# Fourth gated block multiplied ahead of the convolution's sums, and the mean's two products one group sooner

## The chip, the cores and the metric

The kernel runs on one core of a Trainium2 chip. A core has TensorE (matrix products, PE in the profile; its weight loads are listed apart as PEld), VectorE (DVE), ScalarE (ACT), GpSimd (POOL) and SyncE (SP, which issues transfers). The metric is the device time of one execution in microseconds; of several executions the median is given.

## The reference

One block of a streaming encoder, on 512 frames of width 1024: a SwiGLU half step, a mixing layer, another SwiGLU half step, an input gate and a final norm. The change lies in the mixing layer, where two branches are computed from one projection and meet in one output projection:

```python
z = _rmsnorm(h, mix_norm[i]) @ w_in[i]
conv_a, conv_gt, q, k, v, r, g_lr = jnp.split(z, SPLIT_POINTS, axis=-1)
y_conv = _conv_module(conv_a, conv_gt, conv_w[i], conv_b[i], conv_ln_g[i], conv_ln_b[i])
y_gla = _gla(q, k, v, r, g_lr, gate_w_up[i], gate_b[i], gla_norm[i])
h = h + jnp.concatenate([y_conv, y_gla], axis=-1) @ w_out[i]
...
def _conv_module(a, b, w_dw, b_dw, ln_g, ln_b):
    glu = a * jax.nn.sigmoid(b)
    y = lax.conv_general_dilated(glu, w_dw[:, None, :], ...) + b_dw      # causal, depthwise, 31 taps
    return jax.nn.silu(_layernorm(y, ln_g, ln_b))
...
# end of _gla
o = o * lax.rsqrt(jnp.mean(o * o, axis=-1, keepdims=True) + EPS)
o = o * o_norm.astype(f32).reshape(N_HEADS_GLA, HEAD_V)
return (o.reshape(bsz, seq, D_GLA_V) * jax.nn.silu(r.astype(f32))).astype(q.dtype)
```

## The kernel before

Everything is held with channels on the 128 partitions and the 512 frames along the free axis, except where frames stand on the partitions: the values `v`, the gate `r` and the attention's outputs are made in four blocks of 128 frames (`t` = 0 to 3). A product of float32 matrices is done as three products of parts: each operand is split into a high part (a rounded copy, made by ScalarE) and a low part (the rest, made by VectorE), and high x high, low x high and high x low are added up in PSUM.

Within the mixing layer the instructions of each engine run in the order in which they are written (`in_order(True)`): each engine has one queue, and an instruction that waits holds up all behind it. So the order of the lines is the order on the engines.

The lines that matter stand at the end of the mixing layer.

- The loop over `t` from line 1418 makes the gate: `tokblock(wr, t)` projects block `t` on TensorE (24 matmuls of 512 columns), and line 1438 takes its SiLU on ScalarE into `rt[t]`. After `t` = 1 ScalarE also scales the four blocks of the attention's output into `ytok` (line 1449).
- Line 1457 multiplies `ytok[i]` by `rt[i]` on VectorE: block 0 in the turn of `t` = 1, blocks 1 and 2 in that of `t` = 2, block 3 in that of `t` = 3. Between them `taps(n)` (line 1455) puts `n` turns of the convolution on VectorE.
- `taps` (line 1040) takes its turns from one or two generators, `conv_steps` (line 1027), one for each 128 channels of the convolution. A turn is one `scalar_tensor_tensor` over nearly 512 frames, `acc = glu shifted * tap + acc`; a turn that finds a generator at its end issues nothing and drops it. What is left of the taps is issued at line 1485.
- The convolution's four accumulators `acc[0..3]` are added into `acc012` (lines 1453, 1468 and 1489), since the mean over channels needs only their sum.
- Lines 1460 to 1467 transpose the four gated blocks on TensorE into `yps[0..3]`, with six products of another layer (into `pq`) among and behind them. Lines 1470 and 1471 scale and split the transposed blocks (`gsplit`: high part on ScalarE, low part on VectorE) into `mix[4..7]`.
- From there TensorE runs the output projection's half for the attention: `first_part(n, wo[n])` issues 12 matmuls, four groups `k` = 4 to 7 of three. Into `first_part(5, ...)` two products with the constant matrix `mean` are laid, one for the high part `acch` and one for the low part `accl` of `acc012` (line 1490 splits it); they leave the mean over channels, on all partitions, in the bank `mub`.
- Line 1504 subtracts it from the accumulators on VectorE, ScalarE squares them, VectorE adds the squares, and `ln_sums` (called in `first_part(3, ...)` ahead of group 6) sums them over the partitions on TensorE. `ln_out` (called in `first_part(6, ...)` ahead of group 5) spreads the root over the partitions, and the LayerNorm's output goes into `mix[0..3]`, for the other half of the output projection.

Of the kernel before, what the change touches and what calls it, by code (L numbers as in the profile page):

```python
# [12 lines left out]
ALU = mybir.AluOpType  # L13
# [49 lines left out]
def block_kernel(ctx: ExitStack, tc: tile.TileContext, a: dict, out: bass.AP):  # L63
    nc = tc.nc
    pe, dve, act, pool = (Ordered(tc, e) for e in (nc.tensor, nc.vector, nc.scalar, nc.gpsimd))
# [24 lines left out]
    def bt2(dt=F32R, s="a"):  # L90
        t = big.tile([P, 2, SEQ], dt, tag="A", bufs=NA, name=nm(s))
        hi, lo = t[:, 0], t[:, 1]
        whole_of[id(hi)] = hi, t
        return hi, lo

    def bt(dt=F32, s="a"):
        if dt not in other:
            t, other[dt] = bt2(dt, s)
            return t
        return other.pop(dt)  # L100

    def cvt(dt=F32, s="cv"):
        return big.tile([P, SEQ], dt, tag="CV", bufs=NCV, name=nm(s))
# [17 lines left out]
    def psum(pool_, n, shape, tag="mm"):  # L121
        return pool_.tile(shape, F32, tag=tag, bufs=n, name=nm("pd" if len(shape) == 3 else "ps"))

    def singles():
        return region("fixed", "spare" if mode[0] == 0 else stack[1][0] if len(stack) > 1 else "double", "singles")

    def bank():
        if mode[0] == 0:
            turn_no[0] += 1
            at = turn_no[0] % 7  # L130
            if at in (3, 4):
                return fixed()
            if at in (5, 6):
                return spare()
        return psum(singles(), 3, [P, SEQ])

    def fixed():
        return psum(region("fixed"), 2, [P, SEQ])

    def spare():  # L140
        return psum(region("fixed", "spare"), 2, [P, SEQ])
# [10 lines left out]
    def aux():  # L152
        if mode[0] == 2:
            return fixed()
        return psum(singles(), 1, [P, SEQ], "aux")
# [82 lines left out]
    def added(w):  # L238

        h3, l3, r3 = w  # L240
        act.mul(l3, r3, -1.0)
        pool.dma_start(out=l3.bitcast(F32), in_=r3, accum_op=ALU.add)
        return w
# [39 lines left out]
    def rsqrt_mean(ss, n, w, bufs=3, between=None):  # L283

        ms = tmp("ms", 16)[:, :w]
        dve.tensor_scalar(ms, ss, 1.0 / n, EPS, ALU.mult, ALU.add)
        r = tmp("rs0", 16)[:, :w]
        pool.tensor_tensor(out=r, in0=ms, in1=negh[:, :w], op=ALU.pow)
        if between is not None:
            between()  # L290
        nh = tmp("rsh", 16)[:, :w]
        dve.tensor_scalar(nh, ms, -0.5, None, ALU.mult)
        t = tmp("rs1", 16)[:, :w]
        dve.tensor_tensor(out=t, in0=r, in1=r, op=ALU.mult)
        dve.tensor_tensor(out=t, in0=t, in1=nh, op=ALU.mult)
        rs = tmp(f"rs{bufs}", 16, bufs=bufs)[:, :w]
        dve.scalar_tensor_tensor(out=rs, in0=t, scalar=1.5, in1=r, op0=ALU.add, op1=ALU.mult)
        return rs
# [152 lines left out]
    class Left:  # L451
# [17 lines left out]
        def part(self, name, engine=None):  # L469

            if name not in self.done:
                self.done[name] = low(self.cut.pop(name, None) or high(getattr(self, name)), engine or dve)
            return self.done[name]
# [518 lines left out]
    mean, mask, nbias = made  # L992
# [18 lines left out]
    glu, acc, conv = [], [cvt() for _ in range(4)], []  # L1011
# [28 lines left out]
    def taps(n):  # L1040

        for _ in range(n):
            if not conv:
                return
            i = turn[0] % min(2, len(conv))
            turn[0] += 1
            try:
                next(conv[i])
            except StopIteration:
                conv.pop(i)  # L1050
# [187 lines left out]
    def tokblock(w, t, mid={}):  # L1238

        ps = bank()  # L1240
        ts = slice(t * P, (t + 1) * P)
        i = 0
        for k in range(DC):
            wh, wl = w[k // 2][:2]
            xh, xl = hg[k]
            for x, y in ((xh, wh), (xl, wh), (xh, wl)):
                if i in mid:
                    mid[i]()
                pe.matmul(ps, x[:, ts], y[:, k % 2, :], start=(i == 0), stop=(i == 3 * DC - 1))
                i += 1  # L1250
        return ps
# [31 lines left out]
    def chunk_sums(cs):  # L1283
        for j in range(2):
            if len(kvs) == j:
                kvs.append([bank(), bank()])
            for c in cs:
                s0 = (c % 2) * CH
                for i in range(2):
                    h = 2 * j + i  # L1290
                    pe.matmul(kvs[j][c % 2][i * HK:(i + 1) * HK, (c // 2) * HV:(c // 2 + 1) * HV],
                              kdt[j][s0:s0 + CH, (c // 2) * P + i * HK:(c // 2) * P + (i + 1) * HK],
                              vt[c // 2][s0:s0 + CH, h * HV:(h + 1) * HV], start=True, stop=True)
# [18 lines left out]
    def out_of(t, h):  # L1312
        c = 2 * (t % 2) + h // 2
        return ops[2 * (t // 2) + h % 2][:, c * HV:(c + 1) * HV]
# [21 lines left out]
    def chain(cs):  # L1336
        for c in cs:
            for j in range(2):
                state(j, c)
# [39 lines left out]
    def early_parts():  # L1379
        hi, lo = (kept_p[:, i * 2 * P:(i + 1) * 2 * P].rearrange("p (k c) -> p k c", k=2) for i in range(2))  # L1380
        act.copy(hi, early_p)
        added((hi, lo, early_p))
        early_x[:] = [(hi[:, k], lo[:, k]) for k in range(2)]
        wh, wl = (wp.tile([P, 1024], F32R, tag="sm", bufs=2, name=nm("sm")).rearrange("p (k c) -> p k c", k=2)
                  for _ in range(2))
        act.copy(wh, early_w)
        early_wh[:] = added((wh, wl, early_w))[:2]
# [3 lines left out]
    def oload(n):  # L1391
        for i in range(n, n + 2):
            raw_o[i] = load(a["w_out"], 0, DC, i * P, P)

    def ohigh(n):
        return (high4 if n in (4, 5) else high)(raw_o[n])
# [14 lines left out]
    def first_part(n, w, mid={}):  # L1411
        ps = bank()
        part(ps, w, range(4, 8), True, False, mid)
        half[n] = (w, ps)

    oload(0)
    wo, rt = {n: added(ohigh(n)) for n in (0, 1)}, []
    for t in range(TB):
        if t == 0:
            ps = tokblock(wr, t, {5: lambda: chunk_sums(range(7))})  # L1420
            chain(range(7))
            taps(3)
            oload(4)
        elif t == 1:
            ps = tokblock(wr, t, {2: outputs})
            early_parts()
            taps(13)
            by_t = "p (t h) -> p t h"
            so3 = so.rearrange(by_t, h=4)
            dve.tensor_tensor(out=so3, in0=so3, in1=rs2.unsqueeze(2).to_broadcast([P, TB, 4]), op=ALU.mult)  # L1430
            rso = rsqrt_mean(so, HV * HK, 16, between=lambda: taps(5))
            rso3 = rso.rearrange(by_t, h=4)
            dve.scalar_tensor_tensor(out=rso3, in0=rso3, scalar=HK ** -0.5,
                                     in1=rs.unsqueeze(2).to_broadcast([P, TB, 4]), op0=ALU.mult, op1=ALU.mult)
        else:
            ps = tokblock(wr, t)
        r = bt(s="r")
        act.activation(r, ps, AF.Silu, scale=rs[:, t:t + 1])
        rt.append(r)
        if t == 1:  # L1440
            oload(2)
            for n in (4, 5):
                wo[n] = [added(w) for w in ohigh(n)]
            ytok = []
            for i in range(TB):
                y = bt(s="y")
                for h in range(4):
                    vs = slice(h * HV, (h + 1) * HV)
                    act.activation(y[:, vs], out_of(i, h), AF.Copy, scale=rso[:, 4 * i + h:4 * i + h + 1])
                ytok.append(y)  # L1450
        if t == 3:
            acc012 = bt(s="acc012")
            dve.tensor_tensor(out=acc012, in0=acc[0], in1=acc[1], op=ALU.add)
        if t > 0:
            taps((0, 2, 5, 1)[t])
            for i in {1: (0,), 2: (1, 2), 3: (3,)}[t]:
                dve.tensor_tensor(out=ytok[i], in0=ytok[i], in1=rt[i], op=ALU.mult)
    yps = [bank() for _ in range(4)]
    pq = bank()
    for t in range(TB):  # L1460
# [5 lines left out]
    pe.matmul(pq, early_x[0][0], early_wh[1][:, 0, :], start=False, stop=False)  # L1466
    projected(pq, 0, early_wh, early_x, (1,))
    dve.tensor_tensor(out=acc012, in0=acc012, in1=acc[2], op=ALU.add)
    taps(1)
    for h in range(4):  # L1470
        mix[4 + h] = gsplit(yps[h], vec("gla_norm", h), "yg")
    act.copy(kept_pq, pq)
# [12 lines left out]
    for steps in list(conv):  # L1485
        for _ in steps:
# [3 lines left out]
    acch, accl = split(acc012, "sum")  # L1490
# [5 lines left out]
    w1.fetch("a11", "a12")  # L1496
    first_part(4, wo[4])
    mub = aux()
    first_part(5, wo[5], {6: lambda: pe.matmul(mub, mean, acch, start=True, stop=False),
                          7: lambda: pe.matmul(mub, mean, accl, start=False, stop=True)})  # L1500
    first_part(2, wo[2])
    sqs, lln, yc = [], [], []
    for c in range(4):
# [524 lines left out]
```

## Time and profile before

| | us |
|---|---|
| median of 3 runs (921.46 to 922.23) | 922.09 |
| the profiled execution, its own time | 921.7 |
| its span | 920.0 |
| TensorE busy in 450 to 500 us, where the change lies | 49.03 of 50.00 |
| VectorE busy there | 42.34 |
| ScalarE busy there | 32.91 |
| TensorE busy in 500 to 700 us, behind it | 200.00 of 200.00 |

The span runs from the first to the last instruction of the profiled execution; the rest of its time lies around it. A row of the timeline gives start, duration, engine, line, operation, the tile written and the tiles read, and how many instructions are merged into it; in brackets stands how long the engine was idle ahead of it and which engine's instruction ended that. Nearly all instructions go through one helper, so all show its line 46, and tiles are what tells them apart. Tiles are named by the memory that they lie in: two tiles of 512 columns share one name, so that block 0 of `ytok` appears as `r`, blocks 1 to 3 as `y`, the accumulators as `cv`, and `acc012` as `r`.

### The profile page before, as it was taken

The numbers are of one execution on the slowest core, as the hardware profiler recorded it, in microseconds if no ns is written. First come the engines' busy times: TensorE is split into PE (matmuls) and PEld (weight loads), VectorE is DVE, ScalarE is ACT, GpSimd is POOL, SyncE is SP. The second block draws the span as 40 slices with busy tenths as digits, with TensorE's granted clock in tenths as the row PEclk, the third lists the DMA queues.
The fourth block names the chain that finished last, engine by engine and source line by source line (L and its number), as shares of the span: only waits on it lengthen the run. The fifth ranks groups of instructions, "written<-read, shape, count | busy, mean of one in ns | idle before, by whom it ended". The sixth has DMA issues, their size and how long they took to land.

```text
span 920.0 us, 12856 instructions
## 1 busy us (share of the span) xinstructions
PE 910.3 (99%) x4950; PEld 780.1 (85%) x4950; DVE 814.8 (89%) x1087; ACT 517.2 (56%) x755; POOL 63.7 (7%) x80
## 2 busy tenths in 40 slices
PE   9999999999999999999999999999999999999996
PEld 7899888888888887888877889888888888888885
DVE  6699989999989767999996779899999999997896
ACT  7755355445454574484675875455445444556884
POOL 0120000000000111011130020000000000000121
PEclk9999999999999999999999999999999999999998
DMA  9534334224334692267572563334224322358454
GB/s 350 185 96 140 112 112 127 89 74 137 115 91 116 154 273 76 69 122 198 138 166 93 138 160 93 115 116 128 80 90 131 121 92 84 117 155 239 93 98 132
DMA packets 37725, 119.88 MB, mean 130 GB/s; under 512 B 4256, under 2 KB 5536, under 8 KB 37664
## 3 DMA queue, kind: packets, MB, share of 16 engines
q1 hardware_dynamic: 30320, 97.48, 32.3%
q0 software_dynamic: 7200, 21.57, 12.9%
q8 instruction: 39, 0.64, 0.3%
q14 instruction: 22, 0.18, 0.1%
q10 hardware_dynamic: 144, 0.00, 0.0%
HBM read 96.43 MB, written 2.10 MB: 107 GB/s over the span
## 4 chain that ended last, share of the span: by engine, by line
PE 96%; ACT 2%; DVE 1%; DMA 0%; issue 0%; SPq 0%; POOLq 0%
PE ps L46 56%; PE pd L46 40%; DVE cv L46 1%; DMA h<-in_xT 0%; ACT wa L46 0%; ACT sq L46 0%; DVE y L46 0%; ACT r L46 0%; DVE r L46 0%; ACT sm L46 0%; ACT wh L46 0%; DVE hg L46 0%; ACT hg L46 0%; DVE lnsq L46 0%; ACT lnsq L46 0%
## 5 line engine op out<-in xcount | busy, mean ns | idle before, releaser
L46 DVE TENSOR_TENSOR wl<-wr,wh 128x1024 fp32r<-128x1024 f32 (+2 forms) x159 | 186.0, 1180 | 16.8 <-ACT wh L46 16.5
L46 ACT CAST wh<-wr 128x1024 fp32r<-128x1024 f32 (+2 forms) x177 | 175.4, 1023 | 13.3 <-PE ps L46 5.5
L46 PE MATMUL pd<-hg,wh 128*128 128x512 f32 x576 | 150.1, 392 | 0.0
L46 PE MATMUL ps<-act,wh 128*128 128x512 f32 x448 | 138.0, 390 | 0.0
L46 PEld LDWEIGHTS pd<-hg,wh 128*128 128x128 f32 x576 | 106.0, 188 | 21.0 <-DVE u L46 0.4
L46 PE MATMUL ps<-hg,wh 128*128 128x512 f32 (+1 forms) x448 | 116.8, 345 | 0.3
L46 PEld LDWEIGHTS ps<-act,wh 128*128 128x128 f32 x448 | 84.1, 188 | 17.4
L46 PE MATMUL pd<-t,wh 128*128 128x512 f32 x392 | 95.3, 392 | 0.0
L46 ACT ACTIVATE s<-g 128x512 f32<-128x512 f32 x48 | 30.4, 633 | 114.9 <-DVE g L46 114.9
L46 ACT COPY sq<-pd 128x1024 f32<-128x1024 f32 x45 | 45.8, 1017 | 86.7 <-PE pd L46 52.4
L46 PEld LDWEIGHTS ps<-hg,wh 128*128 128x128 f32 x448 | 78.1, 190 | 10.9 <-issue 0.5
L46 PE MATMUL ps<-act,wl 128*128 128x512 f32 x224 | 87.2, 390 | 0.0
L46 PEld LDWEIGHTS pd<-t,wh 128*128 128x128 f32 x392 | 71.5, 189 | 13.4
L46 PE MATMUL pd<-hg,wl 128*128 128x256 f32 (+1 forms) x544 | 81.6, 289 | 0.0
L46 PEld LDWEIGHTS pd<-hg,wl 128*128 128x128 f32 x544 | 73.9, 191 | 5.0
L46 PE MATMUL ps<-hg,wl 128*128 128x512 f32 (+1 forms) x224 | 77.1, 344 | 0.0
L46 ACT CAST wh<-sm 128x1024 fp32r<-128x1024 f32 x42 | 44.0, 1051 | 55.4 <-DVE sm L46 50.1
L46 DVE TENSOR_TENSOR wl<-sm,wh 128x1024 fp32r<-128x1024 f32 x42 | 51.1, 1220 | 5.1 <-ACT wh L46 5.1
L46 DVE TENSOR_TENSOR sq<-pd,sq 128x1024 f32<-128x1024 f32 x45 | 54.8, 1218 | 0.4 <-PE pd L46 0.4
L46 PE MATMUL ps<-wh,hg 128*128 128x512 f32 x176 | 54.5, 391 | 0.0
L46 PE MATMUL pd<-t,wl 128*128 128x256 f32 x392 | 52.5, 283 | 0.0
L46 PEld LDWEIGHTS pd<-t,wl 128*128 128x128 f32 x392 | 50.6, 192 | 1.5
(314 smaller groups left out, 1632.6 us busy)
## 6 DMA issues: line engine op xcount, KB each, us to landing
wr<-in_ffn_w_in SPq DMA_DIRECT2D x84, 512.0 KB, 3.6
wr<-in_ffn_w_out SPq DMA_DIRECT2D x32, 512.0 KB, 3.6
wl<-wr POOLq DMA_DIRECT2D x20, 512.0 KB, 5.7
wr<-in_ffn_w_out SPq DMA_DIRECT2D x16, 384.0 KB, 3.4
wr<-in_w_blocks SPq DMA_DIRECT2D x12, 512.0 KB, 5.4
wr<-in_w_rows SPq DMA_DIRECT2D x8, 512.0 KB, 4.8
wr<-in_w_out SPq DMA_DIRECT2D x8, 512.0 KB, 5.3
wq<-in_ple_w_gate SPq DMA_DIRECT2D x8, 512.0 KB, 4.2
```

The costliest lines, as they stand in the source:

```text
L46: inst = call(*args, **kwargs)
```

## The change

Three edits. Block 3 of the gate's product goes ahead of the first sum over accumulators and of the tap that stood before it; the two first sums then stand one behind the other. One tap is taken from the turn of `t` = 3 to that of `t` = 1, and the tap between the second sum and `gsplit` goes to those that are issued at line 1485. The mean's two products are laid ahead of the groups 5 and 6 of `first_part(5, ...)` instead of 6 and 7. What is computed stays the same, and so does the number of instructions on each engine.

```diff
-        if t == 3:
-            acc012 = bt(s="acc012")
-            dve.tensor_tensor(out=acc012, in0=acc[0], in1=acc[1], op=ALU.add)
         if t > 0:
-            taps((0, 2, 5, 1)[t])
+            taps((0, 3, 5, 0)[t])
             for i in {1: (0,), 2: (1, 2), 3: (3,)}[t]:
                 dve.tensor_tensor(out=ytok[i], in0=ytok[i], in1=rt[i], op=ALU.mult)
+    acc012 = bt(s="acc012")
+    dve.tensor_tensor(out=acc012, in0=acc[0], in1=acc[1], op=ALU.add)
     yps = [bank() for _ in range(4)]
...
     dve.tensor_tensor(out=acc012, in0=acc012, in1=acc[2], op=ALU.add)
-    taps(1)
     for h in range(4):
         mix[4 + h] = gsplit(yps[h], vec("gla_norm", h), "yg")
...
-    first_part(5, wo[5], {6: lambda: pe.matmul(mub, mean, acch, start=True, stop=False),
-                          7: lambda: pe.matmul(mub, mean, accl, start=False, stop=True)})
+    first_part(5, wo[5], {5: lambda: pe.matmul(mub, mean, acch, start=True, stop=False),
+                          6: lambda: pe.matmul(mub, mean, accl, start=False, stop=True)})
```

On VectorE, in the turns of `t` = 1 to 3, this stood before. `cv_3193` to `cv_3196` are the accumulators, a row with `col` is a tap; `r_4291<-r_4291,st_4145` is the product of block 0, `y_4317<-y_4317,r_4291` and `y_4317<-y_4317,y_4326` are those of blocks 1 and 2, `y_4326<-y_4326,r_4391` is that of block 3, and `r_4391<-...cv` are the sums over accumulators:

```order
L46 SCALAR_TENSOR_TENSOR cv_3195<-glu_3522,col,cv_3195 128x511
L46 TENSOR_TENSOR r_4291<-r_4291,st_4145 128x512
L46 SCALAR_TENSOR_TENSOR cv_3196<-en_3578,col,cv_3196 128x501
L46 SCALAR_TENSOR_TENSOR cv_3196<-en_3578,col,cv_3196 128x502
L46 SCALAR_TENSOR_TENSOR cv_3196<-en_3578,col,cv_3196 128x503
L46 SCALAR_TENSOR_TENSOR cv_3196<-en_3578,col,cv_3196 128x504
L46 TENSOR_TENSOR y_4317<-y_4317,r_4291 128x512
L46 TENSOR_TENSOR y_4317<-y_4317,y_4326 128x512
L46 TENSOR_TENSOR r_4391<-cv_3193,cv_3194 128x512
L46 SCALAR_TENSOR_TENSOR cv_3196<-en_3578,col,cv_3196 128x505
L46 TENSOR_TENSOR y_4326<-y_4326,r_4391 128x512
L46 TENSOR_TENSOR r_4391<-r_4391,cv_3195 128x512
```

On VectorE, at the same place, now (block 3's tiles are `y_4326` and `r_4392`):

```order
L46 SCALAR_TENSOR_TENSOR cv_3195<-glu_3522,col,cv_3195 128x511
L46 SCALAR_TENSOR_TENSOR cv_3196<-en_3578,col,cv_3196 128x501
L46 TENSOR_TENSOR r_4291<-r_4291,st_4145 128x512
L46 SCALAR_TENSOR_TENSOR cv_3196<-en_3578,col,cv_3196 128x502
L46 SCALAR_TENSOR_TENSOR cv_3196<-en_3578,col,cv_3196 128x503
L46 SCALAR_TENSOR_TENSOR cv_3196<-en_3578,col,cv_3196 128x504
L46 SCALAR_TENSOR_TENSOR cv_3196<-en_3578,col,cv_3196 128x505
L46 TENSOR_TENSOR y_4317<-y_4317,r_4291 128x512
L46 TENSOR_TENSOR y_4317<-y_4317,y_4326 128x512
L46 TENSOR_TENSOR y_4326<-y_4326,r_4392 128x512
L46 TENSOR_TENSOR r_4392<-cv_3193,cv_3194 128x512
L46 TENSOR_TENSOR r_4392<-r_4392,cv_3195 128x512
```

The tap 501 has moved ahead of block 0's product, and block 3's product stands right behind block 2's, with the first sum and the tap 505 no longer between them.

On VectorE a little later, from the last tap ahead of the four low parts `yg` to the first part of `acc012`, before:

```order
L46 SCALAR_TENSOR_TENSOR cv_3196<-en_3578,col,cv_3196 128x506
L46 SCALAR_TENSOR_TENSOR yg_4425<-ps_4396,col,yg_4425 128x512
L46 SCALAR_TENSOR_TENSOR yg_4428<-ps_4397,col,yg_4428 128x512
L46 SCALAR_TENSOR_TENSOR yg_4431<-ps_4398,col,yg_4431 128x512
L46 SCALAR_TENSOR_TENSOR yg_4434<-ps_4399,col,yg_4434 128x512
L46 SCALAR_TENSOR_TENSOR cv_3196<-en_3578,col,cv_3196 128x507
```

On VectorE, the same place, now:

```order
L46 SCALAR_TENSOR_TENSOR yg_4424<-ps_4396,col,yg_4424 128x512
L46 SCALAR_TENSOR_TENSOR yg_4427<-ps_4397,col,yg_4427 128x512
L46 SCALAR_TENSOR_TENSOR yg_4430<-ps_4398,col,yg_4430 128x512
L46 SCALAR_TENSOR_TENSOR yg_4433<-ps_4399,col,yg_4433 128x512
L46 SCALAR_TENSOR_TENSOR cv_3196<-en_3578,col,cv_3196 128x506
L46 SCALAR_TENSOR_TENSOR cv_3196<-en_3578,col,cv_3196 128x507
```

The tap 506 has moved behind the low parts; five taps stood there (507 to 511), now six, and behind them the last sum.

On TensorE, around the mean's two products (`ps_4511<-sum_4482,mean`; `ps_4512` is the bank of `first_part(5, ...)`, three matmuls a group), before:

```order
L46 MATMUL ps_4512<-yg_4425,wa_4307 128x512 x3
L46 MATMUL ps_4512<-yg_4428,wa_4307 128x512 x3
L46 MATMUL ps_4511<-sum_4482,mean 128x512
L46 MATMUL ps_4512<-yg_4431,wa_4307 128x512 x3
L46 MATMUL ps_4511<-sum_4482,mean 128x512
L46 MATMUL ps_4512<-yg_4434,wa_4307 128x512 x3
```

On TensorE, the same place, now:

```order
L46 MATMUL ps_4512<-yg_4424,wa_4307 128x512 x3
L46 MATMUL ps_4511<-sum_4482,mean 128x512
L46 MATMUL ps_4512<-yg_4427,wa_4307 128x512 x3
L46 MATMUL ps_4511<-sum_4482,mean 128x512
L46 MATMUL ps_4512<-yg_4430,wa_4307 128x512 x3
L46 MATMUL ps_4512<-yg_4433,wa_4307 128x512 x3
```

Each of the two products has moved ahead of one group of three matmuls.

## The prediction

> **What bounds the kernel now.** I read the page's busy shares and its chain of work first, then TensorE's own waits over the whole span, then the timelines of TensorE, VectorE and ScalarE around the two waits that this leaves.
>
> ```profile
> span 920.0 us, 12856 instructions
> PE 910.3 (99%) x4950; PEld 780.1 (85%) x4950; DVE 814.8 (89%) x1087; ACT 517.2 (56%) x755; POOL 63.7 (7%) x80
> PE 96%; ACT 2%; DVE 1%; DMA 0%; issue 0%; SPq 0%; POOLq 0%
> PE ps L46 <- PEq L2018: 0.8, 1, 0.8
> PE ps L46 <- DVE y L46: 0.6, 1, 0.6
> PE ps L46 <- DVE lnsq L46: 0.4, 1, 0.4
> ```
>
> TensorE is busy for 99% of the span and carries 96% of the chain that ended last. Its list of waits (total, times, longest) has three rows: the start of the program, one wait for a `y` of VectorE, one for `lnsq`. So the time falls only where TensorE stands still or does less, and the change takes no matmul away. What can be won is these last two waits.
>
> The first stands at the transposes of the gated blocks, the second at the sums of squares of the LayerNorm.
>
> ```profile
> 469.91 0.39 PE L46 MATMUL ps<-wl,hg 128*128 128x512 f32 x1
> 471.37 0.71 PE L46 MATMUL ps<-sm,up 128*128 128x512 f32 x2
> 472.69 0.66 PE L46 MATMUL ps<-ident,y 128*128 128x128 f32 x4 [0.61 <-DVE y L46]
> 474.12 0.39 PE L46 MATMUL ps<-yg,wh 128*128 128x512 f32 x1
> 474.34 0.40 PE L46 MATMUL ps<-yg,wl 128*128 128x512 f32 x1
> ...
> 489.43 0.39 PE L46 MATMUL ps<-yg,wh 128*128 128x512 f32 x1
> 490.18 1.05 PE L46 MATMUL ps<-ones,lnsq 128*128 128x1 f32 x8 [0.36 <-DVE lnsq L46]
> 491.10 0.49 PE L46 MATMUL ps<-yg,wh 128*128 128x512 f32 x1
> ```
>
> A 512-column matmul shows 0.39 to 0.40 us, but the next one starts 0.22 to 0.23 us after it (474.12, 474.34): starts are what is counted here. The last of the two `sm,up` products starts at 471.37 + 0.71 - 0.39 = 471.69, so the transposes of the fourth block could start at 471.69 + 0.23 = 471.92 and start at 472.69: **0.77 us lost**. The product at 489.43 lets the next start at 489.66; the sums start at 490.18: **0.52 us lost**. Together 1.29 us.
>
> The idle column gives 0.61 + 0.36 = 0.97 us for the same two places. The Trainium skill (Perfetto Trace Analysis, section on the Tensor Engine Instruction) says that a matmul's reported start is the begin of its prefetch and its end is computed from its size, not seen. By that rule the idle column leaves out part of each wait; by the idle column itself the forecast below would be 921.1. The trace agrees with the rule, since starts lie 0.23 us apart under ends that overlap by 0.17.
>
> **The change, part by part.** First, why the transposes wait. VectorE multiplies block after block by its gate; these are its rows, with taps of the convolution (`cv<-...`) between them. In the trace `r<-r,st` is block 0, `y<-y,r` at 469.49 and `y<-y,y` are blocks 1 and 2, `y<-y,r` at 471.95 is block 3, `r<-cv,cv` and `r<-r,cv` are the sums over accumulators.
>
> ```profile
> 464.35 0.74 DVE L46 SCALAR_TENSOR_TENSOR cv<-glu,col,cv 128x511 f32<-128x511 f32 x1
> 465.89 0.69 DVE L46 TENSOR_TENSOR r<-r,st 128x512 f32<-128x512 f32 x1 [0.81 <-ACT r L46]
> 466.50 3.07 DVE L46 SCALAR_TENSOR_TENSOR cv<-en,col,cv 128x501 f32<-128x501 f32 x4
> 469.49 0.68 DVE L46 TENSOR_TENSOR y<-y,r 128x512 f32<-128x512 f32 x1
> 470.09 0.69 DVE L46 TENSOR_TENSOR y<-y,y 128x512 f32<-128x512 f32 x1
> 470.69 0.69 DVE L46 TENSOR_TENSOR r<-cv,cv 128x512 f32<-128x512 f32 x1
> 471.29 0.74 DVE L46 SCALAR_TENSOR_TENSOR cv<-en,col,cv 128x505 f32<-128x505 f32 x1
> 471.95 0.69 DVE L46 TENSOR_TENSOR y<-y,r 128x512 f32<-128x512 f32 x1
> 472.55 0.68 DVE L46 TENSOR_TENSOR r<-r,cv 128x512 f32<-128x512 f32 x1
> 473.15 0.74 DVE L46 SCALAR_TENSOR_TENSOR cv<-en,col,cv 128x506 f32<-128x506 f32 x1
> ...
> 470.34 0.69 ACT L46 ACTIVATE r<-ps,rs 128x512 f32<-128x512 f32 x1 [0.81 <-PE ps L46]
> 473.06 2.42 ACT L46 ACTIVATE yg<-ps,col 128x512 fp32r<-128x512 f32 x4 [2.02 <-PE ps L46]
> ```
>
> *The tap put ahead of block 0's product* costs nothing. VectorE idles for 0.81 us ahead of 465.89; a tap lasts 0.74 and frees the engine 0.65 after its start (464.35 would be followed at 465.01). The tap runs from about 465.0 to 465.75, inside the idle time, and block 0 still starts when ScalarE releases it. Without that cover it would cost 0.65. The four taps and blocks 1 and 2 keep their times.
>
> *Block 3 ahead of the sum and the tap.* VectorE is free for it at 470.69 instead of 471.95. What is late next is its gate: ScalarE's SiLU (470.34, waiting for TensorE's last product of 469.91) ends at 471.03. So block 3 starts at about 471.05 (0.02 for the release, an estimate that nothing hangs on), 0.90 sooner. Before, the transposes followed its start by 472.69 - 471.95 = 0.74; now that gives 471.79, and TensorE's own rhythm 471.92. TensorE becomes the bound; the transposes gain **0.77 us**. If the SiLU ended later than I read, each 0.1 us beyond 0.13 costs 0.1; at the other end nothing more than 0.77 can be won. I take 0.77.
>
> *What follows from it.* ScalarE's four `yg` start 0.37 after the transposes, so at 472.29, and the first low part on VectorE needs its high part (472.29 + 0.7) and VectorE, which is through with both sums at 471.65 + 2 x 0.60 = 472.85. Both are early enough for low parts 0.77 sooner than before, which keeps the products at 474.12 and after at their old distance.
>
> *The sum over the accumulators*, on which the mean waits:
>
> ```profile
> 473.81 2.72 DVE L46 SCALAR_TENSOR_TENSOR yg<-ps,col,yg 128x512 fp32r<-128x512 f32 x4
> 476.45 3.87 DVE L46 SCALAR_TENSOR_TENSOR cv<-en,col,cv 128x507 f32<-128x507 f32 x5
> 480.35 0.69 DVE L46 TENSOR_TENSOR r<-r,cv 128x512 f32<-128x512 f32 x1
> 481.73 0.69 DVE L46 TENSOR_TENSOR sum<-r,sum 128x512 fp32r<-128x512 f32 x1 [0.69 <-ACT sum L46]
> 482.34 1.22 DVE L46 TENSOR_TENSOR wl<-wr,wh 128x1024 fp32r<-128x1024 f32 x1
> 485.10 2.48 DVE L46 TENSOR_TENSOR cv<-cv,ps 128x512 f32<-128x512 f32 x4 [1.54 <-PE ps L46]
> 489.43 0.69 DVE L46 TENSOR_TENSOR lnsq<-lnsq,lnsq 128x512 f32<-128x512 f32 x1 [0.46 <-ACT wh L46]
> 490.04 1.22 DVE L46 TENSOR_TENSOR wl<-wr,wh 128x1024 fp32r<-128x1024 f32 x1
> 491.27 0.16 DVE L46 TENSOR_SCALAR ms<-ps 128x4 f32<-128x4 f32 x1
> ...
> 481.08 0.62 ACT L46 CAST sum<-r 128x512 fp32r<-128x512 f32 x1 [2.28 <-DVE r L46]
> 488.15 1.98 ACT L46 CAST wh<-wr 128x1024 fp32r<-128x1024 f32 x2
> ...
> 483.74 0.40 PE L46 MATMUL ps<-sum,mean 128*128 128x512 f32 x1
> 484.66 0.40 PE L46 MATMUL ps<-sum,mean 128*128 128x512 f32 x1
> 493.29 0.62 PE L46 MATMUL ps<-ident,rs 128*128 128x128 f32 x4
> ```
>
> Five taps, each on the result of the one before, last 3.87, so one step is (3.87 - 0.74) / 4 = 0.78. Now six stand there, from 476.45 - 0.77 = 475.68 (the low parts are sooner by that), and end at 475.68 + 5 x 0.78 + 0.74 = 480.32. The last sum keeps its 480.35, its high part ends on ScalarE at 481.70, its low part on VectorE at 482.42. The sixth tap eats what VectorE won.
>
> *The two products of the mean, one group sooner.* From the first product to the second, 483.74 to 484.66, there are four starts (itself and a group of three), 0.23 each; a group is 0.69. With the 0.77 of above they stand at 483.74 - 1.46 = 482.28 and 484.66 - 1.46 = 483.20. The parts are there at 481.70 and 482.42, so neither waits, with 0.58 and 0.78 to spare. TensorE does the same work in another order: 0 by itself. VectorE's subtraction of the mean came 0.44 after the second product's start (485.10 - 484.66) and had been waited for 1.54; now it can start at 483.64, and the weight part ahead of it ends at 482.34 + 1.22 = 483.56. So **the LayerNorm's chain moves by 1.46 us**, the last product and the engine's readiness nearly together.
>
> *The second wait.* The third sum of squares ends at 489.43 + 0.69 = 490.12, and the column sums start 0.06 behind. Moved by 1.46 they could start at 488.72; TensorE comes there at 489.66 - 0.77 = 488.89. The wait is gone with 0.17 to spare: **0.52 us**. Its 0.46 ahead of 489.43 is put down to a cast of ScalarE; those casts follow the squares without idle time (488.15), so they move along. That is the one release I can't explain: bounds are 1.46 (moves along) and 0 (stands), and I take the first.
>
> *Behind it.* The column sums, the root on POOL and its spread to all partitions (493.29) follow each other closely: nine products lie between 491.10 and 493.29, 0.24 each, so there is at most some 0.1 of waiting, too little for the list. All of it starts from the column sums, thus 1.29 sooner, as TensorE does; and the weight part at 490.04 ends sooner by 1.46, ahead of what reads after it. No new wait. Transfers move too: the weight loads that follow are released by VectorE's and POOL's parts of `wo`, all at the same time or up to 1.46 sooner; TensorE has no wait for a load in its list, so no transfer is at the edge. From 500 us on TensorE has no wait on record, so a shift is kept to the end.
>
> **Sum.** 0.77 + 0.52 = 1.29, so 1.3 us, with 0.1 of doubt at the spread. The profiled execution took 921.7, 1.7 around its span of 920.0; it would take 920.4. It is 0.4 under the median of the runs (922.09, 921.46 to 922.23), and against that the same 1.3 gives **920.8 us**.
>
> **Rivals.**
> *The squares don't move along* (the 0.46 ahead of 489.43 is a release fixed in time). TensorE then gets to 488.89 and stands until 490.18; all is given back there, and the time is 922.1. For it speaks only that the row's releaser doesn't fit the squares; against it, that the casts run right behind them.
> *Only the first wait goes.* If the subtraction starts late, because the low part of the sum or the weight part at 482.34 is late by 0.7, the chain moves by 0.77 only and the 0.52 stays: 921.3. For it: three events lie within 0.2 us of each other there.
> *The mean's low part becomes TensorE's new wait* (the slower side). Its product now stands in a strict queue, with all of the output projection behind it; it comes 1.46 sooner while the part comes no sooner. From 483.20 on, each microsecond of lateness is one of TensorE's. The taps would have to take 0.78 longer to begin with, 0.78 + 1.29 = 2.07 to cancel the gain, and about 3.9 to be 0.2% slower (923.9): six taps of 1.43 instead of 0.78. Against it: no tap in these rows lasts over 0.78.
> *The change doesn't bring block 3 forward*, because its gate ends later than 471.95: then the transposes stay, and only the mean's 0.69 counts, which still takes 0.52 away: 921.6. Against it: the SiLU ends at 471.03.
>
> **How the numbers follow.** Forecast (both waits gone, 920.3 to 921.2 with the runs' scatter of 0.4) 0.70; only one of the two gone (921.3, 921.6) 0.13; the squares stand (922.1) 0.08; the mean's low part late 0.05, most of it by over 0.2%; more won than the two waits, by something that I don't see, 0.04. The range 920.2 to 921.9 holds the forecast and the cases with one wait gone, and with them both bounds of the release but its very end. 0.2% of this time, 1.84 us, is about what a measurement tells from no change; a gain of 1.3 lies within it, so faster 0.08, same 0.86, slower 0.06.
>
> **What would show it.** In the profile after: TensorE's list without the rows for `y` and `lnsq`; the transposes at about 471.9 and block 3 at 471.05 with a short wait for ScalarE ahead of it; a tap inside the old 0.81 of idle time; the sum at 480.35 as before; the mean's products near 482.3 and 483.2; the subtraction near 483.65, the column sums near 488.9. A row "PE ps <- DVE sum" or one still naming `lnsq` would make the forecast wrong, and so would a wait behind 500 us that is not there now.

## The result, and the profile after

| | before | changed |
|---|---|---|
| median, 22 runs each | 921.73 us | 920.32 us |
| lowest to highest | 921.18 to 922.55 | 919.70 to 920.84 |
| ratio (95% interval) | | 0.9983 (0.9977 to 0.9990) |
| profiled execution: own time, span | 921.7, 920.0 | 920.38, 918.7 |

The change makes the kernel 1.41 us faster, or 0.17%; by the interval of the ratio the gain lies between 0.9 and 2.1 us. The slowest run of the changed kernel is under the fastest of the one before.

The busy shares and the chain of the page after, and the whole list of what TensorE waited for in the span:

```profile
span 918.7 us, 12854 instructions
PE 910.2 (99%) x4950; PEld 781.1 (85%) x4950; DVE 815.1 (89%) x1087; ACT 517.2 (56%) x755; POOL 63.7 (7%) x80
PE 99%; DVE 0%; POOLq 0%; ACT 0%; issue 0%
...
PE ps L46 <- PEq L2016: 0.8, 1, 0.8
```

TensorE is as busy as before (910.2 us against 910.3, for 4950 matmuls each time), so it does the same work; the span is shorter by what TensorE no longer stands still. (The page counts 12854 instructions instead of 12856, with equal counts on all engines: the two that are missing are semaphore waits, which are not counted as busy.) The rows for `y` and `lnsq` are gone from its list, and its share of the chain rises from 96% to 99%.

To compare the two executions in the place itself, both are counted from the first transposes there, those of block 0. In the timeline of before they stand at

```profile
470.15 0.60 PE L46 MATMUL ps<-ident,r 128*128 128x128 f32 x4
```

and in TensorE's timeline of the changed kernel 0.34 later, an offset that is there ahead of the place (the tap 511, which no edit touches, starts at 464.35 and 464.71):

```profile
470.49 0.60 PE L46 MATMUL ps<-ident,r 128*128 128x128 f32 x4
472.26 0.60 PE L46 MATMUL ps<-ident,y 128*128 128x128 f32 x4
473.62 0.40 PE L46 MATMUL ps<-yg,wh 128*128 128x512 f32 x1
482.62 0.40 PE L46 MATMUL ps<-sum,mean 128*128 128x512 f32 x1
483.55 0.40 PE L46 MATMUL ps<-sum,mean 128*128 128x512 f32 x1
489.00 0.39 PE L46 MATMUL ps<-yg,wh 128*128 128x512 f32 x1
489.23 0.95 PE L46 MATMUL ps<-ones,lnsq 128*128 128x1 f32 x8
490.04 0.48 PE L46 MATMUL ps<-yg,wh 128*128 128x512 f32 x1
492.24 0.62 PE L46 MATMUL ps<-ident,rs 128*128 128x128 f32 x4
```

None of these rows has brackets any more. Counted from block 0:

| from block 0's transposes to | before | changed | sooner by |
|---|---|---|---|
| block 3's transposes | 2.54 | 1.77 | 0.77 |
| the first product of the output projection | 3.97 | 3.13 | 0.84 |
| the column sums | 20.03 | 18.74 | 1.29 |
| the product behind them | 20.95 | 19.55 | 1.40 |
| the spread of the root | 23.14 | 21.75 | 1.39 |

From 3.13 on the rhythm is TensorE's own: 489.00 to 489.23 is one product's step, where before 0.75 us lay between the same two.

The gain is seen in this stretch alone. In the ten traces of this document the first transposes stand at 469.8 to 470.8, in no order that the edits explain, and from the spread to the end of the span it takes 426.4 to 426.7 us, before, changed and in every experiment.

VectorE's timeline of the changed kernel, and a row of ScalarE's behind it:

```profile
464.71 0.75 DVE L46 SCALAR_TENSOR_TENSOR cv<-glu,col,cv 128x511 f32<-128x511 f32 x1
465.37 0.73 DVE L46 SCALAR_TENSOR_TENSOR cv<-en,col,cv 128x501 f32<-128x501 f32 x1
466.25 0.69 DVE L46 TENSOR_TENSOR r<-r,st 128x512 f32<-128x512 f32 x1 [0.15 <-ACT r L46]
471.41 0.69 DVE L46 TENSOR_TENSOR y<-y,r 128x512 f32<-128x512 f32 x1 [0.27 <-ACT r L46]
472.02 0.69 DVE L46 TENSOR_TENSOR r<-cv,cv 128x512 f32<-128x512 f32 x1
475.98 4.66 DVE L46 SCALAR_TENSOR_TENSOR cv<-en,col,cv 128x506 f32<-128x506 f32 x6
480.68 0.69 DVE L46 TENSOR_TENSOR r<-r,cv 128x512 f32<-128x512 f32 x1
482.06 0.69 DVE L46 TENSOR_TENSOR sum<-r,sum 128x512 fp32r<-128x512 f32 x1 [0.69 <-ACT sum L46]
483.98 2.48 DVE L46 TENSOR_TENSOR cv<-cv,ps 128x512 f32<-128x512 f32 x4
488.32 0.69 DVE L46 TENSOR_TENSOR lnsq<-lnsq,lnsq 128x512 f32<-128x512 f32 x1 [0.46 <-ACT wh L46]
...
470.69 0.69 ACT L46 ACTIVATE r<-ps,rs 128x512 f32<-128x512 f32 x1 [0.79 <-PE ps L46]
```

The idle 0.81 ahead of block 0 has become a tap and 0.15. Block 3 (471.41) waits for its gate, which ScalarE ends at 470.69 + 0.69 = 471.38. The six taps end at 480.64 and the last sum stands at 480.68, which is 480.34 in the times of before: where it stood (480.35). The subtraction of the mean no longer waits 1.54. The third sum of squares still has its 0.46.

### The profile page after: what moved, and what is told of

The parts are those of the page before. It is cut to its first block, busy times and chain, and to the rows that moved or that the text cites. A ratio compares the mean times of both kernels' runs of the same rounds, so it can differ in the third digit from the quotient of the medians.

```text
span 918.7 us, 12854 instructions
## 1 busy us (share of the span) xinstructions
PE 910.2 (99%) x4950; PEld 781.1 (85%) x4950; DVE 815.1 (89%) x1087; ACT 517.2 (56%) x755; POOL 63.7 (7%) x80
## 4 chain that ended last, share of the span: by engine, by line
PE 99%; DVE 0%; POOLq 0%; ACT 0%; issue 0%
PE ps L46 59%; PE pd L46 40%; DVE y L46 0%; POOLq L2022 0%; ACT s L46 0%; DVE u L46 0%; DVE g L46 0%; DVE s L46 0%; DVE rs L46 0%; DVE ms L46 0%; POOLq L46 0%
```

## Experiments

All ratios are to runs of the kernel before on the same chip, with 95% intervals of about 0.0009 to either side. A difference of some tenths of a microsecond between two of these kernels is read from the stretch in TensorE's timeline, from block 0's transposes to the spread: 23.14 us before, 21.75 with the change.

**Block 3 alone.** The change without its last edit:

```diff
-    first_part(5, wo[5], {5: ..., 6: ...})
+    first_part(5, wo[5], {6: ..., 7: ...})
```

> The new order on VectorE, with the mean's two products where they were (ahead of groups 6 and 7). Mine: the wait for y goes and the wait for lnsq stays, since its chain moves only as far as TensorE does: 0.77 us for the transposes and some 0.07 for their restart, so 0.84 us under the kernel before (ratio 0.9991); TensorE's list keeps one row for lnsq of about 0.4, starts 0.5 apart. Rival (the two waits are one, and block 3 carries the whole gain): 1.4 us, no row for lnsq.

920.88 us, ratio 0.9988 (0.9979 to 0.9997). The row of TensorE's list of waits that is left beside the program's start, and its timeline:

```profile
PE ps L46 <- DVE lnsq L46: 0.4, 1, 0.4
...
470.30 0.60 PE L46 MATMUL ps<-ident,r 128*128 128x128 f32 x4
489.56 1.05 PE L46 MATMUL ps<-ones,lnsq 128*128 128x1 f32 x8 [0.36 <-DVE lnsq L46]
492.67 0.62 PE L46 MATMUL ps<-ident,rs 128*128 128x128 f32 x4
```

The row for `y` is gone and that for `lnsq` has kept its 0.36. The stretch is 22.37, 0.77 under that of before. They are two separate waits: block 3 takes away the first and moves the second along whole.

**The mean alone.** The kernel before, with the products ahead of groups 5 and 6:

```diff
-    first_part(5, wo[5], {6: ..., 7: ...})
+    first_part(5, wo[5], {5: ..., 6: ...})
```

> The old order on VectorE, with the mean's two products one group sooner. Mine: the LayerNorm's chain moves by 0.69 us, the 0.52 ahead of the column sums go, with some 0.1 for their restart: 0.5 to 0.6 us under the kernel before (ratio 0.9994); the row for y stays at 0.6. With the run on block 3 alone it adds up to the whole change. Rival (the sum comes too late for products that stand sooner): a row naming sum, and 0 or a loss.

920.89 us, ratio 0.9990 (0.9981 to 0.9999). TensorE's timeline:

```profile
470.54 0.60 PE L46 MATMUL ps<-ident,r 128*128 128x128 f32 x4
473.12 0.66 PE L46 MATMUL ps<-ident,y 128*128 128x128 f32 x4 [0.65 <-DVE y L46]
490.11 0.95 PE L46 MATMUL ps<-ones,lnsq 128*128 128x1 f32 x8
493.12 0.62 PE L46 MATMUL ps<-ident,rs 128*128 128x128 f32 x4
```

Now `lnsq` is gone and `y` has stayed. The stretch is 22.58, 0.56 less (with a first wait 0.04 longer than before, which no edit explains). 0.77 + 0.56 = 1.33 of the 1.39 that both take together: the parts add up to within 0.06. By the medians alone (0.94 and 0.93 under their 921.82, with an uncertainty of 0.8) this could not be said.

**The tap without its cover.** The change, but the tap that went into VectorE's idle time joins those behind the low parts:

```diff
-            taps((0, 3, 5, 0)[t])
+            taps((0, 2, 5, 0)[t])
```

> The whole change, but the tap that was laid into VectorE's idle time ahead of block 0 goes to those behind the low parts, so seven stand there. Mine: block 3 and the transposes keep their gain; the last sum comes 0.78 us later than with the change, the mean's first product waits some 0.2 for its part, the subtraction starts 0.77 later, and 0.4 of the wait for lnsq comes back: 0.6 us over the change, so 0.8 under the kernel before (ratio 0.9992). Rival (a sum that is late is hidden by the slack): as the change, 1.4 under the kernel before.

920.74 us, ratio 0.9987 (0.9978 to 0.9996). VectorE's taps and sum, then TensorE's timeline:

```profile
476.24 5.43 DVE L46 SCALAR_TENSOR_TENSOR cv<-en,col,cv 128x505 f32<-128x505 f32 x7
481.70 0.69 DVE L46 TENSOR_TENSOR r<-r,cv 128x512 f32<-128x512 f32 x1
...
470.74 0.60 PE L46 MATMUL ps<-ident,r 128*128 128x128 f32 x4
483.10 0.50 PE L46 MATMUL ps<-sum,mean 128*128 128x512 f32 x1
489.90 1.05 PE L46 MATMUL ps<-ones,lnsq 128*128 128x1 f32 x8
493.01 0.62 PE L46 MATMUL ps<-ident,rs 128*128 128x128 f32 x4
```

Seven taps last 5.43 instead of 4.66. The last sum comes 10.96 after block 0's transposes instead of 10.19: 0.77 late. The mean's first product is late by 0.23 (12.36 against 12.13), the column sums by 0.42 (19.16 against 18.74), the spread by 0.52 (22.27 against 21.75). TensorE's list has no row for these waits; the starts show them. So the slack does not hide a late sum, and the tap's place is part of the change. I had expected 0.6.

**What ends the 0.46 ahead of the third sum of squares.** The prediction left this release unexplained; the row names a cast of ScalarE. Block 3 alone keeps the wait for `lnsq`, so there an earlier third sum shows in TensorE. First, with the two casts ahead of the squares:

```diff
+    for n in (6, 7):
+        wo[n] = ohigh(n)
     sqs, lln, yc = [], [], []
...
-    for n in (6, 7):
-        wo[n] = ohigh(n)
```

> As the run with block 3 alone (the mean's products at their old place), and the casts of the weights 6 and 7 ahead of the four squares on ScalarE, in its idle time. It asks what ends the 0.46 us ahead of the third sum of squares. If it is the cast, as the row has it: the third sum comes 0.46 sooner and the wait for lnsq shrinks from some 0.5 to under 0.1, 0.4 us under the run with block 3 alone. If it is anything else: the 0.46 and the wait stay, and the time is that of block 3 alone.

920.58 us, ratio 0.9990 (0.9981 to 0.9999). VectorE's third sum, then TensorE's timeline:

```profile
488.31 0.69 DVE L46 TENSOR_TENSOR lnsq<-lnsq,lnsq 128x512 f32<-128x512 f32 x1 [0.46 <-DVE lnsq L46]
...
469.79 0.60 PE L46 MATMUL ps<-ident,r 128*128 128x128 f32 x4
492.17 0.62 PE L46 MATMUL ps<-ident,rs 128*128 128x128 f32 x4
```

With no cast near it (both end at 483.22, 5 us earlier), the 0.46 is the same, and the row now names the second sum. The stretch is 22.38, as with block 3 alone (22.37). The cast was not the cause.

Then, with the sums in pairs. In a row of three, the second and the third sum each wait for ScalarE (their square) and for VectorE (the sum before); in pairs each waits for one of them. The program's list of VectorE's waits, for the row of three and for the pairs:

```
lnsq_4541<-lnsq_4541 [waits Activation]
lnsq_4541<-lnsq_4541,lnsq_4546 [waits DVE,Activation] x2
...
lnsq_4541<-lnsq_4541 [waits Activation]
lnsq_4546<-lnsq_4546 [waits Activation]
lnsq_4541<-lnsq_4541,lnsq_4546 [waits DVE]
```

The edit:

```diff
-    for c in range(1, 4):
-        dve.tensor_tensor(out=sqs[0], in0=sqs[0], in1=sqs[c], op=ALU.add)
+    for i, j in ((0, 1), (2, 3), (0, 2)):
+        dve.tensor_tensor(out=sqs[i], in0=sqs[i], in1=sqs[j], op=ALU.add)
```

> As the run with block 3 alone (the mean's products at their old place, so the wait for lnsq is there), with the three sums of squares in pairs: 0+1, 2+3, then the two results. No sum then waits for both ScalarE and the sum before it, as the second and third do in a row of three. It asks again what ends the 0.46 us ahead of the third sum. If it is the double wait: the 0.46 goes, the column sums start with TensorE's rhythm, the row for lnsq goes, and from the first transposes to the spread it takes 0.5 to 0.6 us less than with block 3 alone, as with the whole change. If it is the third sum in itself or its operands: the 0.46 stays ahead of it, and so does TensorE's row.

920.50 us, ratio 0.9987 (0.9978 to 0.9996). VectorE's three sums, then TensorE's timeline:

```profile
487.04 1.48 DVE L46 TENSOR_TENSOR lnsq<-lnsq 128x512 f32<-128x512 f32 x2
488.55 0.69 DVE L46 TENSOR_TENSOR lnsq<-lnsq,lnsq 128x512 f32<-128x512 f32 x1
...
470.48 0.60 PE L46 MATMUL ps<-ident,r 128*128 128x128 f32 x4
488.98 0.39 PE L46 MATMUL ps<-yg,wh 128*128 128x512 f32 x1
489.30 1.05 PE L46 MATMUL ps<-ones,lnsq 128*128 128x1 f32 x8
492.41 0.62 PE L46 MATMUL ps<-ident,rs 128*128 128x128 f32 x4
```

The third sum follows the second by 488.55 - 488.52 = 0.03. TensorE's row for `lnsq` is gone, and the stretch is 21.93, 0.44 under block 3 alone. It is not quite TensorE's rhythm yet: the column sums could start at 488.98 + 0.23 = 489.21 and start at 489.30, and that 0.09 with a restart of 0.1 is the distance to the change's 21.75.

So the 0.46 goes with the row of three, and the pairs remove it. That the double wait itself costs 0.46 is not shown, and other rows speak against it. The second sum in a row of three has the same two waits and follows by 0.10 only. In another norm of the kernel before, VectorE adds ScalarE's squares (`sq`) to a sum (`sqacc`) four times in a row, and each add from the second on waits for the add before it and for ScalarE too (whose square is done in time):

```profile
348.90 3.08 DVE L46 TENSOR_TENSOR sqacc<-sqacc,sq 128x512 f32<-128x512 f32 x4
```

The step there is (3.08 - 0.69) / 3 = 0.80, so each add follows the end of the one before by some 0.10. In these places the two waits thus cost 0.10, and what adds 0.36 at this third sum stays open. The pairs also give the third sum another operand (the sum of squares 2 and 3 instead of square 3), and this run doesn't separate that from the waits.

**The change with sums in pairs**, to see whether the chain behind still holds anything back:

> The whole change with the same pairwise sums. Mine: TensorE has no wait left that this could take away, so it only adds some 0.4 us to the slack of 0.2 ahead of the column sums: from the first transposes to the spread as with the change, within 0.1 us, and the time too. Rival (the root and the spread behind the column sums are still bound by the LayerNorm's chain): 0.2 us or more under the change.

920.12 us, ratio 0.9985 (0.9976 to 0.9994). TensorE's timeline:

```profile
470.72 0.60 PE L46 MATMUL ps<-ident,r 128*128 128x128 f32 x4
492.47 0.62 PE L46 MATMUL ps<-ident,rs 128*128 128x128 f32 x4
```

The stretch is 21.75, to the hundredth that of the change. More slack brings nothing, and this version is no faster than the change by anything that was measured.

**The mean's products still sooner.** First ahead of groups 4 and 5 instead of 5 and 6:

```diff
-    first_part(5, wo[5], {5: ..., 6: ...})
+    first_part(5, wo[5], {4: ..., 5: ...})
```

> The whole change, with the mean's two products two groups sooner than before instead of one (ahead of groups 4 and 5). Mine: the first product then stands at 481.9 in the times of the changed kernel's profile and its part ends at 482.02, so TensorE waits 0.1 there; the chain behind is not late, so nothing is won: within 0.15 us of the change, a touch over it. Rival (an earlier mean wins more, the chain still bounds): 0.3 us or more under the change.

920.38 us, ratio 0.9986 (0.9977 to 0.9995). TensorE's timeline:

```profile
470.57 0.60 PE L46 MATMUL ps<-ident,r 128*128 128x128 f32 x4
482.16 0.51 PE L46 MATMUL ps<-sum,mean 128*128 128x512 f32 x1
482.50 0.87 PE L46 MATMUL ps<-yg,wa 128*128 128x512 f32 x3
492.59 0.62 PE L46 MATMUL ps<-ident,rs 128*128 128x128 f32 x4
```

One group sooner (0.69) would be 11.44 after block 0's transposes; the product starts at 11.59, a wait of 0.15, and the next one 0.34 behind it instead of 0.23. The stretch is 22.02, 0.27 over that of the change: the wait (0.15) and its restart (0.11), no more. The medians are too coarse to show it.

Then ahead of the last two groups of the output block before, the slower rival made real:

```diff
-    first_part(4, wo[4])
     mub = aux()
-    first_part(5, wo[5], {5: ..., 6: ...})
+    first_part(4, wo[4], {6: ..., 7: ...})
+    first_part(5, wo[5])
```

> The whole change, with the mean's two products ahead of the last two groups of the output block before (three groups sooner than in the change). Mine, the slower rival made real: the first product waits for its part from 480.55 to 482.04, 1.5 us in which all of the output projection stands behind it; TensorE's list gets a row for sum of over 1 us, and the time is 1.4 to 1.5 us over the change, about that of the kernel before. Rival (the wait is given back, since the LayerNorm's chain comes sooner too): as the change, within 0.3.

921.67 us, ratio 1.0001 (0.9992 to 1.0010); beside the run with two groups, on the same chip, 1.29 us more. The row of TensorE's list of waits that is left beside the program's start, and its timeline:

```profile
PE ps L46 <- ACT sum L46: 1.3, 1, 1.3
...
470.81 0.60 PE L46 MATMUL ps<-ident,r 128*128 128x128 f32 x4
479.56 1.52 PE L46 MATMUL ps<-yg,wa 128*128 128x512 f32 x6
482.39 0.50 PE L46 MATMUL ps<-sum,mean 128*128 128x512 f32 x1 [1.32 <-ACT sum L46]
491.19 0.94 PE L46 MATMUL ps<-ones,lnsq 128*128 128x1 f32 x8
```

The last of the six products starts at 479.56 + 1.52 - 0.39 = 480.69, the next could start at 480.92 and starts at 482.39: 1.47 lost, of the 1.5 expected. The column sums come 20.38 after block 0's transposes, 1.64 later than with the change: the wait, its restart and 0.06. Nothing is given back, and the whole gain is gone. Here a wait in TensorE's queue costs its whole length.

## Why the prediction was right, and where it was wrong

*The mechanism and its places* were right, and each event stands where the prediction put it. Taking 0.34 from the times of the changed kernel: block 3 at 471.07 (predicted 471.05), its transposes at 471.92 (471.92), the last sum at 480.34 (480.35), the mean's products at 482.28 and 483.21 (482.28 and 483.20), the subtraction at 483.64 (483.64), the column sums at 488.89 (488.89).

*The tap put ahead of block 0* costs nothing, as reckoned; the run in which it stands behind the low parts instead prices the place at 0.5 us.

*The two waits* are separate terms, as the two halves show: 0.77 of 0.77 for the first, 0.56 for the second where 0.52 stood in the sum.

*Counting by starts* was the better choice. The Trainium skill (Perfetto Trace Analysis, Tensor Engine Instruction) says that a matmul's reported end is computed from its size and not observed. The measured numbers agree with counting by starts: these promised 1.29, the idle column 0.97, and the stretch lost 1.39.

*The sum was 0.1 short.* It counted the gaps and had no term for the restarts behind them. What comes first after a wait takes longer than in TensorE's rhythm: the four transposes and the four products behind them take 1.36 us now, where it was 1.43 after a wait (472.26 to 473.62 against 472.69 to 474.12), and the column sums 0.81 instead of 0.92. That is 0.18; 0.07 of it goes into a longer way between the two places (15.61 us against the 15.54 that are left of before without its wait).

*The step that failed is the last one, how the numbers follow.* The prediction said that 0.2%, 1.84 us, is "about what a measurement tells from no change; a gain of 1.3 lies within it", and so put 0.86 on "same" and 0.08 on "faster". That term, the smallest change that a measurement can tell, was about three times too large for runs of this number, and no row was given for it. Single runs scatter by up to 0.8 us around their median, but 22 of each give the ratio to within 0.0007 to either side, about 0.6 us: 0.9983, with an upper end of 0.9990, and the two sets of runs do not overlap. A gain of 1.41 us is under 0.2% and still clearly told from none; the prediction's own forecast of 1.3 would have been, too.

*The time itself*, 920.32, lies 0.5 under the 920.8 predicted and near the lower end of the range. Of that, 0.1 is the larger gain and 0.4 is the level: the kernel before has a median of 921.73 over 22 runs, where the three runs at hand had 922.09. It stayed inside the range because that was 1.7 us wide: the error of the level was three times that of the gain.

*The rivals.* The squares moved along (the third sum starts 1.45 sooner, at 487.98 in the times of before), so that rival fell: the release is not fixed in time, and it was not a cast. The slower rival missed by 0.6 to 0.8 us: by so much the parts of the sum were there ahead of the mean's two products. But it is real: the run with the two products four groups sooner than before paid for its 1.47 us of wait in full.

*What stays open*: why the third sum of squares in a row of three is delayed by 0.46, when the second, and the adds of another norm, with the same two waits are delayed by 0.10. The gain does not hang on it, since the 0.46 moved along whole.

## What to carry to other kernels

Where one engine is busy for 99%, list its few waits, measure each by starts rather than by the idle column, and ask of each which instruction on the releasing engine could stand earlier without anything new ahead of it: here it was enough to move a product of one block, two taps and two matmuls. An instruction may go sooner in a strict queue up to the moment at which its operand is there, and not further; three groups sooner than the change cost all that the change had won. Work that must yield its place goes where its engine already idles, and the gap is read from the row that follows it.

## What was not expected of the hardware

- The third sum of squares on VectorE started 0.46 us after the end of the second in every run in which the three stood in a row (before, changed, and the six experiments that left them so), with ScalarE's casts near it or 5 us earlier. In pairs, where it waits for the sum before it alone, it was 0.03 us. With the same two waits, the second of the three took 0.10, and so did the adds into `sqacc`.
- A wait of TensorE cost 0.07 to 0.11 us beyond its gap: 0.07 at block 3's transposes, 0.11 at the column sums. The first 512-column product behind a wait shows 0.50 to 0.51 us instead of 0.39 to 0.40, and the next starts 0.34 us behind it instead of 0.23 (482.39 to 482.73 with the four groups, 482.16 to 482.50 with the two).
- A tap that uses the result of the tap before took a step of 0.78 us ((4.66 - 0.74) / 5 for the six, (5.43 - 0.74) / 6 for the seven), while taps that alternate between two accumulators took 0.66 (464.71 to 465.37 in the changed kernel).
